# A hybrid attention / delta-rule layer on one core: streams woven in longer runs, two weight loads hoisted further, products of a constant at the start

## The chip, the cores and the metric

The kernel runs on one core of a Trainium2 chip. Its engines are TensorE (PE in the profile, with its weight loads as PEld), VectorE (DVE), ScalarE (ACT), GpSimd (POOL) and the engine whose queue issues most DMAs (SP). Each engine takes its instructions in the order in which the program lists them for that engine and waits where one needs a result of another. The metric is the device time of one execution in microseconds (us), lower is better.

## The reference

One layer over T = 1024 tokens of width D = 1024, all in float32. The input is normalised and multiplied by one wide matrix; its columns feed two mixers that run beside each other, and two gates merge them.

```python
h = rms_norm(x, pre_w)
proj = h @ w_in
# A: stick-breaking attention, 8 heads x 64, blocks of 128 queries
z = jnp.einsum('bhqd,bhkd->bhqk', qb, kb) * scale
log_keep = jnp.where(causal, -jax.nn.softplus(z), 0.0)
suffix = lax.cumsum(log_keep, axis=3, reverse=True) - log_keep
a = jnp.where(causal, jnp.exp(jax.nn.log_sigmoid(z) + suffix), 0.0)
o = jnp.einsum('bhqk,bhkd->bhqd', a, vb)
# B: conv(4) + SiLU on q, k, v, then a gated delta rule, 4 heads x 128, in chunks with a scan over them
merged = (jax.nn.sigmoid(merge_sb) * (o_sb @ w_branch_sb)
          + jax.nn.sigmoid(merge_gdn) * (o_g @ w_branch_gdn))
y = merged @ w_out
return x + rms_norm(y, post_w)
```

## The kernel before

**Dense tiles.** A product with a block of 128 columns of a weight matrix is made in two halves of 512 tokens. Weights and activations are split into a high and a low part, and of the four partial products three are made, over 8 blocks of the inner dimension: 24 matmuls of 512 columns for a half, into one of three PSUM tiles ("d"). `dense` (lines 204 to 214) is a generator that gives control back after every 3 matmuls and says that they cost 0.64. All other PSUM tiles, five of them, share one ring ("g"): the attention's scores z, transposes aT and results av are among them.

**Weights.** `load_w` (92 to 94) issues the DMA of a weight block (`raw`), ScalarE's copy that gives the high part (`whi`) and VectorE's subtraction that gives the low part (`wlo`). `tc.high_priority(offset=WPRI)` puts these three forward by 200 places of the program in the eyes of the framework's scheduler, which then fixes the order of each engine. Each of the three has two buffers.

**The stages by time.** 0 to 58 us: the rows of x are normalised, transposed on TensorE (xT, line 262), split into h_hi (ScalarE, 268) and h_lo (VectorE, 269), and the first two projections d_k (201) are made as the quarters of h become ready. 58 to 185 us: projections and preparation of the delta rule's first two heads (`g_mid(0)`); in its second half VectorE runs `lanes` (line 655 calls it), a chain of 62 dependent instructions (tmp, line 433, and a sum, line 435) whose size grows from one step to the next, and beside it TensorE makes dense tiles from `fill` (the merge gates, d_mg) and `g_gate` (d_gg). 185 to 245 us: the first scan, woven with two dense tiles. 245 to 368 us: `g_mid(1)`, the same for the other two heads, its lanes from about 306 to 356 us. 368 to 421 us: the second scan, woven with d_sk and d_sv. 421 to 489 us: more dense tiles and the branch product d_yb. 489 to 829 us: the attention, in four passes of two heads. 829 to 972 us: the branch product d_ya, the output product y (923), the last normalisation.

**The attention.** For every group of two query blocks `sb_z` (735 to 759) makes the scores in pieces of up to 512 columns (two matmuls each, 751 and 752); ScalarE makes two sigmoids of every piece (kp, bt; 754 and 755), VectorE runs a scan along kp (757) and GpSimd multiplies (758). `sb_av` (761 to 805), one group later, transposes blocks of bt (aT, line 774: four 128x128 transposes into one PSUM tile), has VectorE (779, 781) or ScalarE (783) copy them out, and multiplies pairs of blocks by the values (av, line 788), always one pair behind the transposes, except for a group's last pair. `weave` (233 to 243) joins this stream with the dense tiles of the next pass: at every step it runs the stream whose share of its stated cost is the smaller one, until that stream yields once.

Of the kernel before, what the change touches and what calls it, by code (L numbers as in the profile page):

```python
# [17 lines left out]
P = 128  # L18
# [2 lines left out]
CAP = 60.0  # L21
NSLOT = 23
AB = 4


@with_exitstack
def tile_stickbreak_gdn_hybrid(
# [15 lines left out]
    nc = tc.nc  # L43
# [3 lines left out]
    NP = 4  # L47
# [20 lines left out]
    def gps(name, shape=None):  # L68
        return psg.tile(shape or [P, 512], F32, tag="g", name=name)
# [20 lines left out]
        return hi, lo  # L90

    def load_w(src, nk, name):
        with tc.high_priority(offset=WPRI):
            return split_w(load_raw(src, nk, name), nk, name)

    WPRI = 200

    xs = []
    raw0 = []
# [52 lines left out]
    def rsqrt_act(dst, src, scale, bias, bias_f):  # L152
# [7 lines left out]
        nc.vector.tensor_mul(dst, dst, t)  # L160
        return sq

    epsb = const.tile([P, 1], F32, name="epsb")
    nc.vector.memset(epsb, EPS)
    prev_sq = [None]
# [58 lines left out]
    def chain(*gens):  # L224
        for g in gens:
            yield from g

    def drain(*gens):
        for g in gens:
            for _ in g:  # L230
                pass

    def weave(main, main_cost, side, side_cost):
        done = [0.0, 0.0]
        tot = [main_cost, side_cost]
        gens = [main, side]
        live = [True, True]
        while live[0] or live[1]:
            i = 0 if live[0] and (not live[1] or done[0] / tot[0] <= done[1] / tot[1]) else 1
            try:  # L240
                done[i] += next(gens[i])
            except StopIteration:
                live[i] = False

# [9 lines left out]
    for q in range(4):  # L254
        if q < 3:
            stats(q + 1)
        for k2 in range(NK // 2):
            ps = gps(f"xT_{q}_{k2}")
            for kk in range(2):
                for j in range(2):  # L260
                    k = k2 * 2 + kk
                    nc.tensor.transpose(ps[:, (kk * 2 + j) * P:(kk * 2 + j + 1) * P],
                                        xs[2 * q + j][:, k * P:(k + 1) * P], ident)
            qs = slice(q * QT, (q + 1) * QT)
            for kk in range(2):
                k = k2 * 2 + kk
                pk = ps[:, kk * QT:(kk + 1) * QT]
                ev = nc.scalar.mul(h_hi[:, k, qs], pk, prew[:, k:k + 1])
                nc.vector.scalar_tensor_tensor(h_lo[:, k, qs], pk, prew[:, k:k + 1], h_hi[:, k, qs].bitcast(F32),
                                               op0=ALU.mult, op1=ALU.subtract)  # L270
        if q < 2:
            hi = wp.tile([P, NK, P], F32R, tag="whi", name=f"whi_{first[q][1]}")
            lo = wp.tile([P, NK, P], F32R, tag="wlo", name=f"wlo_{first[q][1]}")
            nc.gpsimd.tensor_scalar(hi, raw0[q], 1.0, 1.0, op0=ALU.mult, op1=ALU.mult)
            nc.gpsimd.tensor_tensor(lo, raw0[q], hi.bitcast(F32), op=ALU.subtract)
            w0.append((hi, lo))
        todo = [(0, q)] if q < 2 else ([(1, 0), (1, 1), (0, 2), (1, 2)] if q == 2 else [(0, q), (1, q)])
        for i, qq in todo:
            ps = psd.tile([P, QT], F32, tag="d", name=f"d_{first[i][1]}_{qq}")
            dense_mm(ps, w0[i], NK, hk, qq * QT, (qq + 1) * QT)  # L280
            nc.scalar.copy(pre0[i][:, qq * QT:(qq + 1) * QT], ps)
# [140 lines left out]
    def lanes(b, lane_in):  # L422
        L = slot(f"L{b}", shape=[64, 32, 32])
        nc.sync.dma_start(L, lane_in.rearrange("h r c i j -> (h r c) i j"))
        nc.vector.tensor_scalar(L, L, -1.0, None, op0=ALU.mult)
        XL = slot(f"XL{b}", shape=[64, 32, 32])
        nc.gpsimd.memset(XL, 0.0)
        nc.gpsimd.affine_select(out=XL, in_=XL, pattern=[[1, 32], [-1, 32]], compare_op=ALU.not_equal, fill=1.0,
                                base=0, channel_multiplier=0)
        tmp = slot(f"tmp{b}")  # L430
        for i in range(1, 32):
            tv = tmp[:64, :i * i].rearrange("p (c j) -> p c j", j=i)
            nc.vector.tensor_tensor(tv, XL[:, 0:i, 0:i].rearrange("p j c -> p c j"),  # L433
                                    L[:, i:i + 1, 0:i].broadcast_to([64, i, i]), op=ALU.mult)
            nc.vector.tensor_reduce(XL[:, i, 0:i], tv, axis=AX.X, op=ALU.add)
        last = nc.vector.tensor_copy(L, XL.rearrange("p i j -> p j i"))
        lx = dram.tile([2, 4, NT, 32, 32], F32, name=f"lane_x{b}")
        lxt = dram.tile([2, 4, NT, 32, 32], F32, name=f"lane_xt{b}")
        nc.sync.dma_start(lx.rearrange("h r c i j -> (h r c) i j"), XL)
        nc.sync.dma_start(lxt.rearrange("h r c i j -> (h r c) i j"), L)  # L440
        lane_out[b] = lx, lxt
        return last
# [180 lines left out]
    def fill(n):  # L623
        for _ in range(n):
            if not gates:
                return
            m = gates.pop(0)
            wg = load_w(win[:, 4104 + m * P:4104 + (m + 1) * P], NK, f"mg{m}")
            gt = slot(f"mg_{m}")
            for half in range(2):  # L630
                hs = slice(half * HT, (half + 1) * HT)
                ps = yield from dense(wg, NK, hk, half, f"mg{m}")
                nc.scalar.activation(gt[:, hs], ps, AF.Sigmoid)  # L633
            nc.sync.dma_start(mg_d[m], gt)

    def g_mid(b, prev):
        h0, h1 = 2 * b, 2 * b + 1
        bs = slice(b * 16, b * 16 + 16)
        drain(g_q(h0))
        for h in (h0, h1):  # L640
            kn[h] = slot(f"kn_{h}", shape=[P, NT, P])
            sumsq(kT[h], ssk, h, f"k{h}", kn[h])
        li = g_m(b)
        drain(g_q(h1))
        for h in prev:
            g_o(h)
        sumsq(qT[h0], ssq, h0, f"q{h0}")
        g_i(h0)
        drain(g_v(h0))
        drain(g_v(h1))  # L650
        sumsq(qT[h1], ssq, h1, f"q{h1}")
        rsqrt(rqs[:, bs], ssq[:, bs], 1.0, 16)
        nc.vector.tensor_scalar(rqs[:, bs], rqs[:, bs], float(P) ** -0.5, None, op0=ALU.mult)
        g_i(h1)
        last = lanes(b, li)
        drain(fill(1))
        g_vt(h0)
        drain(fill(1))
        g_vt(h1)
        drain(fill(2), g_gate(h0), g_gate(h1))  # L660
        return chain(g_lev(h0, last), g_lev(h1, last), g_scan((h0, h1)))

    gates = gates[8:] + gates[:8]
# [175 lines left out]
    def until_none(g):  # L839
        for v in g:  # L840
            if v is None:
                return
            yield v

    for p in range(NP):
        side = chain(*[f(p + 1) for f in stages], fill(1)) if p + 1 < NP else fill(4)
        weave(until_none(att), 24.0, side, 52.0 if p + 1 < NP else 41.0)
    drain(fill(16), att)


# [120 lines left out]
```

## Time and profile before

| | |
|---|---|
| median of 3 runs | 977.01 us (977.01, 977.5, 972.46) |
| the profiled execution | 974.01 us |
| its span in the trace | 972.3 us |
| PE busy | 932.6 us, 96% of the span |
| VectorE, ScalarE, GpSimd busy | 628.3, 391.7, 192.6 us |
| attention, 489.3 to 829.4 us | 340.1 us, PE busy 333.2 us |

The span is what the trace covers; 1.7 us of the profiled execution lie around it. "Busy" leaves out waits. A row of the timeline gives the start of an instruction in us from the span's start and its length; a PE row's length includes the time in which it overlaps the next one, so the price of a matmul is read from start to start. In brackets stands how long the engine had been idle before it and what released it.

### The profile page before, as it was taken

To read this page: it belongs to the slowest core of one execution; us is meant where nothing else is said; L and a number is where in the kernel's file an instruction comes from. 1 tells how busy PE (TensorE), PEld (TensorE's weight loads), DVE (VectorE), ACT (ScalarE), POOL (GpSimd) and SP (SyncE) were. 2 spreads that over 40 slices of the span, in tenths; PEclk is the share of its full clock that TensorE was granted. 3 is DMA by queue.
4 is the path that set the end of the run, shared out by engine and by line. 5 is a ranking of instruction groups with operands and counts; after the bars stand their busy time and mean duration, and the time that the engine had idled before them with its cause. 6 is when DMAs were issued, how large, how long until landed. Compare 5 with 4: busy or idle time off the path is not lost.

```text
span 972.3 us, 13372 instructions
## 1 busy us (share of the span) xinstructions
PE 932.6 (96%) x5134; PEld 748.4 (77%) x5134; DVE 628.3 (65%) x1066; ACT 391.7 (40%) x861; POOL 192.6 (20%) x117
## 2 busy tenths in 40 slices
PE   4999999899999989999999999999999999999997
PEld 4968787688887767887887777777777777777886
DVE  6666899656899974656466635783774674563244
ACT  5665531235655212443254433552453443232221
POOL 4010210001103000000034312540632362341000
PEclk9999999999999989999999999999999999999999
DMA  8014222400242142004730111020011202671152
GB/s 262 7 41 118 77 65 86 110 23 23 66 109 66 66 112 40 12 23 155 246 109 22 44 44 43 22 66 23 22 43 44 77 33 65 246 269 70 46 196 106
DMA packets 88418, 80.12 MB, mean 82 GB/s; under 512 B 17097, under 2 KB 74530, under 8 KB 88354
## 3 DMA queue, kind: packets, MB, share of 16 engines
q1 hardware_dynamic: 86944, 79.20, 26.2%
q8 instruction: 40, 0.66, 0.3%
q10 hardware_dynamic: 1410, 0.07, 0.1%
q14 instruction: 24, 0.20, 0.1%
HBM read 60.88 MB, written 18.37 MB: 82 GB/s over the span
## 4 chain that ended last, share of the span: by engine, by line
PE 75%; DVE 15%; issue 4%; ACT 3%; POOL 2%; DMA 1%; SPq 0%; DVEq 0%; POOLq 0%; ACTq 0%
PE d_mg L211 12%; PE y L923 8%; PE d_sk L211 5%; PE d_sq L211 5%; PE d_sv L211 5%; PE d_yb L211 4%; PE d_q L211 4%; PE d_sgt L211 4%; PE av L788 4%; DVE tmp L433 3%; PE aT L774 3%; PE d_k L211 2%; PE d_gg L211 2%; PE d_k L201 2%; DVE kp L757 2%
## 5 line engine op out<-in xcount | busy, mean ns | idle before, releaser
L758 POOL TENSOR_TENSOR bt<-bt,kp 128x127 f32<-128x127 f32 (+3 forms) x64 | 123.1, 1941 | 381.0 <-DMA mb<-mg_d 164.9
L757 DVE TENSOR_TENSOR_SCAN kp<-kp,mscan 128x128 f32<-128x128 f32 (+3 forms) x64 | 105.5, 1673 | 30.2 <-ACT kp L754 29.9
L211 PE MATMUL d_mg<-h_hi,whi_mg 128*128 128x512 f32 x256 | 104.7, 409 | 0.2 <-ACT mg L633 0.2
L211 PE MATMUL d_mg<-h_hi,wlo_mg 128*128 128x512 f32 x256 | 100.8, 394 | 0.0
L211 PE MATMUL d_mg<-h_lo,whi_mg 128*128 128x512 f32 x256 | 100.1, 391 | 0.0
L754 ACT ACTIVATE kp<-z 128x384 f32<-128x384 f32 (+4 forms) x96 | 47.8, 499 | 71.6 <-PE z L752 67.3
L211 PEld LDWEIGHTS d_mg<-h_hi,whi_mg 128*128 128x128 f32 x256 | 48.2, 188 | 11.5 <-issue 3.4
L211 PEld LDWEIGHTS d_mg<-h_hi,wlo_mg 128*128 128x128 f32 x256 | 48.1, 188 | 10.5 <-issue 0.2
L211 PEld LDWEIGHTS d_mg<-h_lo,whi_mg 128*128 128x128 f32 x256 | 48.2, 188 | 7.6
L923 PE MATMUL y<-wohi,m_hi 128*128 128x512 f32 (+1 forms) x136 | 52.0, 383 | 1.2 <-ACT m_hi L879 1.2
L755 ACT ACTIVATE bt<-z 128x384 f32<-128x384 f32 (+4 forms) x96 | 47.7, 498 | 11.7 <-DMA mB_d<-mb 5.4
L923 PE MATMUL y<-wohi,m_lo 128*128 128x512 f32 (+1 forms) x136 | 52.0, 382 | 0.4 <-DVE m_lo L880 0.4
L923 PE MATMUL y<-wolo,m_hi 128*128 128x512 f32 (+1 forms) x136 | 51.8, 381 | 0.0
L433 DVE TENSOR_TENSOR tmp<-XL,L 64x1 f32<-64x1 f32 (+30 forms) x62 | 47.7, 769 | 1.6
L788 PE MATMUL av<-aT,svn 128*64 128x256 f32 (+1 forms) x320 | 39.6, 370 | 6.7 <-DVE aT L779 3.6
L774 PEld LDWEIGHTS aT<-ident,bt 128*128 128x128 f32 x288 | 35.6, 140 | 10.4 <-issue 0.8
L774 PE MATMUL aT<-ident,bt 128*128 128x128 f32 x288 | 43.5, 273 | 0.2 <-ACT bt L755 0.2
L356 POOL TENSOR_TENSOR acc_k<-acc_k,pre_k 128x1024 f32<-128x1024 f32 x4 | 9.6, 2390 | 157.9 <-ACT pre_k L355 136.9
L788 PEld LDWEIGHTS av<-aT,svn 128*64 128x64 f32 x320 | 19.8, 136 | 25.6 <-issue 15.5
L927 ACT ACTIVATE yj<-y 128x512 f32<-128x512 f32 (+1 forms) x17 | 9.7, 573 | 66.9 <-PE y L923 64.4
L211 PE MATMUL d_gg<-h_hi,wlo_gg 128*128 128x512 f32 x64 | 26.5, 414 | 9.4 <-DVE wlo_gg L89 9.4
L895 POOL TENSOR_TENSOR sA<-sA,mBl 128x512 f32<-128x512 f32 x16 | 24.7, 1557 | 47.8 <-DVE sA L894 45.7
(377 smaller groups left out, 2468.6 us busy)
## 6 DMA issues: line engine op xcount, KB each, us to landing
raw_mg<-in_w_in_dram SPq DMA_DIRECT2D x16, 512.0 KB, 4.0
mg_d<-mg SPq DMA_DIRECT2D x16, 512.0 KB, 3.0
x<-in_x_dram SPq DMA_DIRECT2D x8, 512.0 KB, 6.4
mb<-mg_d SPq DMA_DIRECT2D x8, 512.0 KB, 6.8
mB_d<-mb SPq DMA_DIRECT2D x8, 512.0 KB, 4.2
sA<-mg_d SPq DMA_DIRECT2D x8, 512.0 KB, 7.2
mBl<-mB_d SPq DMA_DIRECT2D x8, 512.0 KB, 6.1
rawo<-in_w_out_dram SPq DMA_DIRECT2D x8, 512.0 KB, 4.6
```

Of the source, the lines that this page charges most:

```text
L201: nc.tensor.matmul(ps, lhsT=a[:, k], rhs=b[:, c0:c1], start=(k == 0 and i == 0), stop=(k == nk - 1 and i == 2))
L211: nc.tensor.matmul(ps, lhsT=a[:, k], rhs=b[:, hs], start=(k == 0 and i == 0), stop=(k == nk - 1 and i == 2))
L433: nc.vector.tensor_tensor(tv, XL[:, 0:i, 0:i].rearrange("p j c -> p c j"), L[:, i:i + 1, 0:i].broadcast_to([64, i, i]), op=ALU.mult)
L754: nc.scalar.activation(kp[:, os_], ps[:, :pc], AF.Sigmoid, scale=-0.125)
L755: nc.scalar.activation(bt[:, os_], ps[:, :pc], AF.Sigmoid, scale=0.125)
L757: nc.vector.tensor_tensor_scan(kp[:, :n], kp[:, :n], mscan[:, :n], 1.0, op0=ALU.mult, op1=ALU.max)
L758: nc.gpsimd.tensor_tensor(bt[:, 1:n], bt[:, 1:n], kp[:, 0:n - 1], op=ALU.mult)
L774: nc.tensor.transpose(ps[:, (a * 2 + j) * P:(a * 2 + j + 1) * P], at[p, a, qb][:, off:off + P], ident)
L788: nc.tensor.matmul(av[a * 64:(a + 1) * 64, j0 * P:2 * P], lhsT=vn[:, c, a * 64:(a + 1) * 64], rhs=aT[:, a * 2 + j0:a * 2 + 2], start=(c == ...
L895: nc.gpsimd.tensor_tensor(ga[:, hs], ga[:, hs], mb[:, hs], op=ALU.add)
L923: nc.tensor.matmul(ps, lhsT=a[:, k, ts_], rhs=b[:, c0:c1], start=(k == 0 and i == 0), stop=(k == NK - 1 and i == 2))
L927: nc.scalar.activation(junk.rearrange("p a b -> p (a b)")[:, :c1 - c0], ps, AF.Square, accum_out=ss)
```

## The change

It has three parts. First, `weave` takes two numbers, and lets a stream go on until it has done that much more of its stated cost: 1.9 for both streams in the two scans; in the attention 1.9 for the attention's own stream and 5.0 for the dense one, which is a whole half of a dense tile (8 x 0.64 = 5.12). Second, `load_w` reads its offset from `ahead`; in `g_mid` it is 600 instead of 200 between the call of `lanes` and the end of the dense tiles beside it. Third, `keep_awake` multiplies a 128x128 matrix of ones by itself into a PSUM tile that nothing reads: 18 times at the beginning, and 6 times each behind two of the first quarter's four groups of transposes.

```diff
+RUN = 1.9
+HALF = 5.0
...
     def load_w(src, nk, name):
-        with tc.high_priority(offset=WPRI):
+        with tc.high_priority(offset=ahead[0]):
             return split_w(load_raw(src, nk, name), nk, name)
 
-    WPRI = 200
+    ahead = [200]
...
+    def keep_awake(n, after=None):
+        with ExitStack() as held:
+            if after is not None:
+                held.enter_context(tc.issue_after(after.ins))
+            ps = gps("awake")
+            for i in range(n):
+                nc.tensor.matmul(ps[:, :P], lhsT=ones, rhs=ones, start=True, stop=True)
+
+    keep_awake(18)
...
-    def weave(main, main_cost, side, side_cost):
+    def weave(main, main_cost, side, side_cost, runs=(RUN, RUN)):
...
             try:
-                done[i] += next(gens[i])
+                upto = done[i] + runs[i]
+                while done[i] < upto:
+                    done[i] += next(gens[i])
             except StopIteration:
                 live[i] = False
...
                     k = k2 * 2 + kk
-                    nc.tensor.transpose(ps[:, (kk * 2 + j) * P:(kk * 2 + j + 1) * P],
+                    xt_ = nc.tensor.transpose(ps[:, (kk * 2 + j) * P:(kk * 2 + j + 1) * P],
                                         xs[2 * q + j][:, k * P:(k + 1) * P], ident)
+            if q == 0 and k2 % 2:
+                keep_awake(6, xt_)
...
         last = lanes(b, li)
+        ahead[0] = 600
         drain(fill(1))
...
         drain(fill(2), g_gate(h0), g_gate(h1))
+        ahead[0] = 200
...
-        weave(until_none(att), 24.0, side, 52.0 if p + 1 < NP else 41.0)
+        weave(until_none(att), 24.0, side, 52.0 if p + 1 < NP else 41.0, (RUN, HALF))
```

The lines of the attention lie 17 further down in the changed kernel (774 is 791, 788 is 805, 751 is 768), those of `dense` 11 (211 is 222).

On TensorE, in a pass of the attention beside the dense tile d_mg, the order before has a product of three between the transposes of one block (aT_2_4) and the products av of the pair before:

```order
L774 MATMUL aT_2_4_5779<-ident,bt_0_4_5443 128x128
L774 MATMUL aT_2_4_5779<-ident,bt_0_5_5479 128x128
L774 MATMUL aT_2_4_5779<-ident,bt_1_4_5502 128x128
L774 MATMUL aT_2_4_5779<-ident,bt_1_5_5522 128x128
L211 MATMUL d_mg_1_5752<-h_hi,whi_mg_5683 128x512
L211 MATMUL d_mg_1_5752<-h_lo,whi_mg_5683 128x512
L211 MATMUL d_mg_1_5752<-h_hi,wlo_mg_5684 128x512
L788 MATMUL av_2_5740<-aT,svn_4866 64x256 x4
```

Here is the same place on TensorE in the changed kernel, from the last matmul of a dense half on:

```order
L222 MATMUL d_mg_1_5799<-h_hi,wlo_mg_5731 128x512
L791 MATMUL aT_2_4_5824<-ident,bt_0_4_5479 128x128
L791 MATMUL aT_2_4_5824<-ident,bt_0_5_5493 128x128
L791 MATMUL aT_2_4_5824<-ident,bt_1_4_5507 128x128
L791 MATMUL aT_2_4_5824<-ident,bt_1_5_5521 128x128
L805 MATMUL av_2_5776<-aT,svn_4913 64x256 x4
L791 MATMUL aT_2_3_5835<-ident,bt_0_4_5479 128x128
L791 MATMUL aT_2_3_5835<-ident,bt_0_5_5493 128x128
```

All 24 matmuls of the half now stand ahead of aT_2_4, and none between it and av. Over the attention, TensorE's list before has 396 unbroken stretches of one kind (dense, scores, transposes, av), of which 38 are av blocks; after, 159, of which 32 are av blocks. Of the 40 pairs of av, 11 had less than 1.4 us of TensorE work between their own last transposes and them before and the others 2.5 to 6 us; after, 14 have less than 2.3 us and the other 26 have 5.9 us or more (counted in the two orders, with the start-to-start times of the trace). Runs of scores reach 7 pieces, four times.

On VectorE, near the end of the second lanes (tmp and the sum XL, of growing size), the order before puts the low part of the fourth head's gate weights behind the last sum:

```order
L433 TENSOR_TENSOR tmp_2925<-XL_2920,L_2917 64x900
L435 TENSOR_REDUCE XL_2920<-tmp_2925 64x30
L433 TENSOR_TENSOR tmp_2925<-XL_2920,L_2917 64x961
L435 TENSOR_REDUCE XL_2920<-tmp_2925 64x31
L89 TENSOR_TENSOR wlo_gg_3324<-raw_gg_3321,whi_gg_3323 128x1024
L436 COPY L_2917<-XL_2920 64x1024
```

The changed kernel has VectorE make it two instructions earlier:

```order
L448 TENSOR_TENSOR tmp_2958<-XL_2953,L_2950 64x900
L450 TENSOR_REDUCE XL_2953<-tmp_2958 64x30
L91 TENSOR_TENSOR wlo_gg_3357<-raw_gg_3354,whi_gg_3356 128x1024
L448 TENSOR_TENSOR tmp_2958<-XL_2953,L_2950 64x961
L450 TENSOR_REDUCE XL_2953<-tmp_2958 64x31
L451 COPY L_2950<-XL_2953 64x1024
```

The third head's wlo_gg moves in the same way, from behind the sum of size 26 to between tmp of size 625 and the sum of size 25. In the first lanes the two keep their places.

On TensorE at the start, the order before goes from the last transposes of the first quarter (x_85 and x_87 are its two tiles) to three products of d_k, and then on to the second quarter's first transpose (x_91):

```order
L262 MATMUL xT_3_227<-ident,x_85 128x128
L262 MATMUL xT_3_227<-ident,x_87 128x128
L201 MATMUL d_k_0_240<-h_hi,whi_k_236 128x256
L201 MATMUL d_k_0_240<-h_lo,whi_k_236 128x256
L201 MATMUL d_k_0_240<-h_hi,wlo_k_237 128x256
L262 MATMUL xT_0_292<-ident,x_91 128x128
```

The changed kernel has six products of ones there, and then d_k without a transpose between its products:

```order
L275 MATMUL xT_3_253<-ident,x_85 128x128
L275 MATMUL xT_3_253<-ident,x_87 128x128
L171 MATMUL awake<-ones 128x128 x6
L212 MATMUL d_k_0_273<-h_hi,whi_k_269 128x256
L212 MATMUL d_k_0_273<-h_lo,whi_k_269 128x256
L212 MATMUL d_k_0_273<-h_hi,wlo_k_270 128x256
```

All 24 products of d_k's first quarter now precede the second quarter's 16 transposes, which before lay among them. Six more products of ones stand between the first quarter's second and third group of transposes, 18 ahead of everything. In the two scans TensorE's order is the same in both kernels; GpSimd's order is the same throughout.

## Rows read from the trace of the kernel before

**Rows 1.** The page's head and its first part: busy time, share of the span and number of instructions of each engine.

```profile
span 972.3 us, 13372 instructions
PE 932.6 (96%) x5134; PEld 748.4 (77%) x5134; DVE 628.3 (65%) x1066; ACT 391.7 (40%) x861; POOL 192.6 (20%) x117
```

**Rows 2.** The table of stretches: start and end, length, then busy us and number of instructions of PE, PEld, DVE, ACT and POOL, the clock that TensorE was granted (1.00 is the upper of its two levels), the DMA engines' share and GB/s. A stretch behind the second lanes, and the attention.

```profile
353.70:360.60 6.90, 5.44 (x13) 4.28 (x14) 5.31 (x7) 0.00 (x0) 0.00 (x0) 0.51 0.67 159
489.30:829.40 340.10, 333.23 (x1776) 258.86 (x1774) 206.17 (x203) 148.82 (x294) 119.71 (x59) 1.00 0.16 48
```

**Rows 3.** The table of waits of the whole span: who waited for whom, us in total, times, the longest.

```profile
PE d_gg L211 <- DVE wlo_gg L89: 9.4, 4, 3.8
...
PE av L788 <- DVE aT L779: 3.6, 3, 1.4
...
PE av L788 <- DVE aT L781: 3.1, 2, 1.8
...
PEld av L788 <- issue: 15.5, 26, 2.2
```

**Rows 4.** The timeline of PE alone, at one av block that stands between dense matmuls, and at the attention's very end, where av and transposes follow each other.

```profile
516.62 0.39 PE L211 MATMUL d_sv<-h_lo,whi_sv 128*128 128x512 f32 x1
516.85 0.39 PE L211 MATMUL d_sv<-h_hi,wlo_sv 128*128 128x512 f32 x1
517.16 1.08 PE L788 MATMUL av<-aT,svn 128*64 128x256 f32 x8
518.18 0.50 PE L211 MATMUL d_sv<-h_hi,whi_sv 128*128 128x512 f32 x1
518.52 0.40 PE L211 MATMUL d_sv<-h_lo,whi_sv 128*128 128x512 f32 x1
...
823.88 1.08 PE L788 MATMUL av<-aT,svn 128*64 128x256 f32 x8
824.89 1.09 PE L774 MATMUL aT<-ident,bt 128*128 128x128 f32 x8
...
827.74 1.74 PE L788 MATMUL av<-aT,svn 128*64 128x256 f32 x16
829.40 0.50 PE L211 MATMUL d_ya<-oshi,whi_wbs 128*128 128x512 f32 x1
```

**Rows 5.** The timeline of all engines around one wait of av in the third pass: the low part of a weight and a scan on VectorE, the transposes, the copy, and av.

```profile
597.13 1.66 DVE L89 TENSOR_TENSOR wlo_sq<-raw_sq,whi_sq 128x1024 fp32r<-128x1024 f32 x1 [0.51 <-ACT whi_sq L88]
...
598.71 2.03 DVE L757 TENSOR_TENSOR_SCAN kp<-kp,mscan 128x512 f32<-128x512 f32 x1
...
599.02 0.38 PE L774 MATMUL aT<-ident,bt 128*128 128x128 f32 x2
...
600.66 0.99 DVE L779 TENSOR_TENSOR aT<-aT,mdiag 128x512 f32<-128x512 f32 x2
...
601.47 0.76 PE L788 MATMUL av<-aT,svn 128*64 128x256 f32 x6 [1.36 <-DVE aT L779]
```

**Rows 6.** The attention's groups of the same line and shape, 489.3 to 829.4 us: count, busy us, mean ns of one, idle before. The scores' two sigmoids of 384 columns; then, of line 757, all scans with the shortest, median and longest in ns.

```profile
L754 ACT ACTIVATE kp<-z 128x384 f32<-128x384 f32 x23 | 11.5, 502 | 15.0 <-PE z L752 14.9
L755 ACT ACTIVATE bt<-z 128x384 f32<-128x384 f32 x23 | 11.5, 499 | 0.0
...
L757 DVE TENSOR_TENSOR_SCAN kp<-kp,mscan x59: 418/1731/4411, 494.0 to 800.1; 128x512 f32<-128x512 f32 x8, 128x640 f32<-128x640 f32 x8, 128x768 f32<-128x768 f32 x8, 128x896 f32<-128x896 f32 x8
```

**Rows 7.** The timeline of VectorE and of PE in the second lanes.

```profile
334.53 1.31 DVE L433 TENSOR_TENSOR tmp<-XL,L 64x625 f32<-64x625 f32 x1
...
338.94 1.21 DVE L89 TENSOR_TENSOR wlo_gg<-raw_gg,whi_gg 128x1024 fp32r<-128x1024 f32 x1
...
340.20 0.50 PE L211 MATMUL d_gg<-h_hi,wlo_gg 128*128 128x512 f32 x1 [1.30 <-DVE wlo_gg L89]
...
349.85 1.08 DVE L435 TENSOR_REDUCE XL<-tmp 64x30 f32<-64x900 f32 x1
...
353.89 1.21 DVE L89 TENSOR_TENSOR wlo_gg<-raw_gg,whi_gg 128x1024 fp32r<-128x1024 f32 x1
...
355.16 0.79 PE L211 MATMUL d_gg<-h_hi,wlo_gg 128*128 128x512 f32 x1 [3.78 <-DVE wlo_gg L89]
355.75 0.63 PE L211 MATMUL d_gg<-h_hi,whi_gg 128*128 128x512 f32 x1
...
360.44 0.46 PE L211 MATMUL d_gg<-h_hi,wlo_gg 128*128 128x512 f32 x1
360.75 0.40 PE L211 MATMUL d_gg<-h_hi,whi_gg 128*128 128x512 f32 x1
```

**Rows 8.** The timeline of the start: the row of x that the first transposes wait for, those transposes, d_k's wait and the last transposes of the second quarter. The last two rows are of the first scan: a product of two 128x128 float32 matrices, which the trace shows as two records, and the instruction behind it.

```profile
9.48 2.94 DVE L179 TENSOR_SCALAR x<-x,rx 128x1024 f32<-128x1024 f32 x1
...
12.48 2.82 PE L262 MATMUL xT<-ident,x 128*128 128x128 f32 x12 [3.44 <-DVE x L179]
...
17.91 0.38 PE L201 MATMUL d_k<-h_lo,whi_k 128*128 128x256 f32 x1 [1.73 <-DVE h_lo L269]
...
21.28 0.93 PE L262 MATMUL xT<-ident,x 128*128 128x128 f32 x7
...
205.64 0.38 PE L554 MATMUL Sn<-vs,kn 128*128 128x128 f32 x2
205.85 0.39 PE L549 MATMUL vnew<-vb,Xt 128*128 128x128 f32 x2
```

## The prediction

> **What bounds the kernel now.** I read the busy table first. TensorE works 932.6 of 972.3 us, and no other engine comes near [rows 1]: so a microsecond counts only where TensorE waits, or where it is slower than it could be. The table of waits shows where it waits [rows 3]: 9.4 us in four waits for the low part of a gate weight (d_gg), 6.7 us in five waits of av for VectorE's copies of the transposes (3.6 and 3.1). The last row there is of the weight loads: before 26 of av's 320, the loader stood still for 15.5 us with nothing to wait for. The table of stretches adds the clock [rows 2]: it is at the upper level in the attention, and 0.51 in the 6.9 us behind the second lanes. Of the attention's 340.1 us TensorE is busy 333.2; the rest is nearly all av's five waits.
>
> **The attention: fewer switches.** A step in a dense run is 0.23 us (516.62 to 516.85) [rows 4]. The block of eight av between 516.85 and 518.52 takes 1.67 us with two dense steps in it, so 1.67 - 2 x 0.23 = 1.21 us. What the eight need by themselves comes from the attention's end: eight take 1.01 us (823.88 to 824.89), sixteen, of which four are half as wide, 1.66 us (827.74 to 829.40), so six full ones more take 0.65 us, 0.108 each, and eight 0.87. Coming from dense work and going back to it thus costs 1.21 - 0.87 = 0.34 us. The order has 38 av blocks before and 32 after: 6 x 0.34 = **2.0 us less**. The many fewer switches between dense work and scores or transposes I count at nothing: I found no such loss at them in the rows. The ends of this term are 2.0 and, by the row of the loader (15.5 us in 26 blocks, 0.6 each), 3.6 us.
>
> [...]
>
> **The attention: av's old waits.** One of the five [rows 5]: the transposes are done at 599.4, but VectorE has a weight's low part (1.66 us) and a scan (2.03 us) in hand, begins the copy at 600.66, and av starts at 601.47, 1.36 us late. There was little between the transposes and av. Now a whole dense half of 24 x 0.23 = 5.5 us stands ahead of 26 of the 40 pairs of av. The same queue (1.66 + 2.03 us) and the copy (0.99 us) make 4.7 us, less than that. So these waits go: **6.7 us less**; bounds 0 and 6.7.
>
> **The attention: what is late next.** Three things. (1) 14 pairs keep less than 2.3 us of cover, three more than before had less than 1.4; each with one scan ahead of its copy (median 1.73 us [rows 6]) could wait up to about 1 us. (2) Runs of scores are longer. A piece of 384 columns needs two sigmoids of 0.50 us on ScalarE [rows 6], where TensorE makes it in some 0.35 us (two matmuls, three quarters of a dense step each). With five PSUM tiles in the ring, one of them held by av, a piece can start when the fourth before it has been read: the sixth waits until 0.35 + 2 x 1.0 = 2.35 us instead of 1.75, the seventh until 3.35 instead of 2.70, together 1.25 us. Four such runs cost 5 us, and 2.6 if the two sigmoids overlap a little (0.8 us a piece). (3) GpSimd and VectorE get their work in bursts, but the results are wanted only one group later. I take **3 us more**, near the lower price of the runs, and keep 0 and 8 (5 of the runs, 3 of the short covers) as ends. The attention together: -2.0 - 6.7 + 3 = -5.7 us, and from -10 to +6 between the ends.
>
> **The second lanes.** For the third head, VectorE begins wlo_gg at 338.94 and TensorE starts at 340.20, 1.30 us late, so it was there at 338.90. Now wlo_gg follows tmp of size 625, which ends at 335.84 [rows 7]; it is ready at 337.1: this wait goes, 1.3 us. For the fourth head, wlo_gg now follows the sum that ends at 350.93, not the one at 353.9, and is ready at 352.15. TensorE came to it at 355.16 - 3.78 = 351.38, and with the 1.3 us won, at 350.08; it waits 2.1 us instead of 3.8. It starts at 352.2 in place of 355.16: **2.9 us less**, both waits together. VectorE's chain itself ends at the same time as before, since it only takes the two subtractions earlier; what depends on its end (the loads of the lanes' result) is not later. Queued behind the two subtractions are the chain's next steps, 1.2 us later each, and nothing else waits for those. Then the clock: from 355.75 to 360.44 a step takes 0.43 us and from 360.75 on 0.23, in the stretch with clock 0.51 [rows 2, 7]. That is 13 steps at 0.2 us, 2.6 us. Whether a wait of 2.1 us brings the same drop no row shows: I take half, **1.3 us less**, with ends 0 and 2.6. The term is -4.2; its ends are -5.5, and 0 if the scan behind it, which needs the lanes' result, waits for what was won. The two waits in the first lanes (the rest of the 9.4 us) stay, since the order there is unchanged.
>
> **Hoisting on the queues.** The higher offset issues a handful of loads on SP's queue one place earlier. SP's queue has nothing there that TensorE waits for [rows 3], so I count nothing; bounds of -0.5 and +0.5.
>
> **The start.** The 18 first products stand ahead of work that waits for x: TensorE's first long row begins at 12.48, after 3.44 us idle behind VectorE's 2.94 us row [rows 8]. A product of two float32 matrices of 128x128 takes 0.21 us (205.64 to 205.85), and twice that at the lower level: 18 are 3.8 to 7.6 us, and fit into the idle time. The other 12 products lie on the path: 2.5 us, or 5.0 at the lower level. Against that stand the 1.73 us for which d_k waited for h_lo at 17.91, which the products now partly fill, so 0.8 to 3.3 us more. If TensorE were at its upper level already at 12.48, the first quarter's 14 remaining transposes would take 0.13 us each as in the row at 21.28 (0.93 for 7) instead of 0.23 (2.82 for 12), 1.4 us less: the lower end is -0.6. The second quarter's transposes now come behind all of d_k's first quarter, and with them ScalarE's and VectorE's split of that quarter; TensorE has d_k's other tile for the first quarter to do meanwhile (24 products), so I count nothing for it, with +1 as its end. I take **1.5 us more**, with ends -0.6 and +4.3.
>
> **The sum**, against the profiled execution (974.0 us, 972.3 in the span): -5.7 - 4.2 + 1.5 = -8.4, so 965.6 us. That execution is 3.0 us below the median of the runs shown, and the four times average 975.2; the like of that average is **967 us**.
>
> **Rivals.** (a) *The gain stays away.* The attention's waits only change their place: av's copies come late for the 14 short covers and the scores wait for PSUM, in all as much as the 6.7 us before. Then -2.0 + 3 (runs) + 0, lanes -2.9 without the clock, start +2.5: +0.6, about 976. For it speaks that VectorE is 61% busy in the attention (206.2 of 340.1 us [rows 2]), against it that 26 pairs get a cover longer than the queue seen at a wait. (b) *Slower: VectorE's bursts.* With scores in runs, two or three scans stand together in VectorE's queue, in front of the copies for av. The longest scan took 4.41 us [rows 6]; two such and a low part of 1.66 us are 10.5 us, 5 us more than the dense half covers. It decides from about 5.5 us of queue on. Once in each pass would be 4 x 5 = 20 us: -8.4 - 3 + 20 = +8.6, about 984. Against it speaks that the longest is two and a half times the median. [...] (d) *The products at the start don't do what they are named for:* they leave the clock as it was and cost their whole 4.3 us; 970 with the rest as forecast.
>
> **How the numbers follow.** A measurement of this kernel can tell about 0.5%, 4.9 us, from no change: faster is below 972.1, slower above 981.9. Forecast 0.50, (a) 0.26, (b) 0.11, (c) 0.05, (d) 0.08. The forecast's own range is 961 to 972, from the lanes' and the attention's middle ends. (c) and (d) are also faster, if little: with a quarter of (d) and a tenth of the forecast going to "same", faster has 0.45 + 0.05 + 0.06 = 0.56; same 0.05 + 0.02 + 0.24 of (a) = 0.31; slower (b) and the rest of (a), 0.13. The range is 958 to 979: the good ends of attention and lanes below, (a) with a bad start above; (b) lies outside.
>
> **What would show it.** In the changed profile: av's waits for aT gone or below 2 us in the table of waits (else (a)); no wait of av above 3 us (else (b)); the third head's wait for wlo_gg gone and the fourth's near 2.1 us, and whether the clock behind it stays up; scores waiting for ScalarE, 3 us in all; d_k's first product behind the last products of ones at about 16 to 18 us, and h ready 1 to 2 us later. The forecast is wrong if the attention takes more than 337 us, or if the start loses more than 4 us.

## The result and the profile after

The changed kernel takes 980.12 us (median of 8 runs, 978.11 to 982.7), against 975.31 us for the kernel before in the same comparison (8 runs): the ratio is 1.0058 with a 95% interval of [1.0042, 1.0074]. It is slower by 0.6%, where I had forecast 967 us and a range up to 979. The profiled execution took 980.29 us.

The page's head and first part of the changed kernel answer to [rows 1]:

```profile
span 978.6 us, 13475 instructions
...
PE 942.0 (96%) x5194; PEld 763.8 (78%) x5194; DVE 626.1 (64%) x1066; ACT 386.7 (40%) x861; POOL 192.6 (20%) x117
```

The span is 6.3 us longer; TensorE is busy 9.4 us more. Of these, 7.8 us lie before the logits, where the change gives TensorE 60 more records, the 30 products of ones, and 2.5 us in the attention, where the number of records is the same. A matmul at the lower clock is longer, and so counts as more busy time: a step of d_mg takes 0.23 us at 312.36 us, where the clock is 1.00, and 0.43 at 317.43, where it is 0.50. The busy share hides such a loss. The table of waits of the changed kernel's TensorE answers to [rows 3]:

```profile
PE av L805 <- DVE aT L796: 6.9, 5, 2.5
PE d_gg L222 <- DVE wlo_gg L91: 4.2, 2, 2.6
...
PE d_mg L222 <- ACT mg L648: 3.9, 1, 3.9
PE t_q L379 <- ACT jk L381: 2.2, 1, 2.2
PE av L805 <- DVE aT L798: 2.0, 3, 0.9
...
PE aT L791 <- ACT bt L772: 1.1, 2, 0.7
```

The waits for wlo_gg fell from 9.4 to 4.2 us, but a wait of d_mg for ScalarE is new (3.9), one of t_q grew from 0.8 to 2.2, and av waits 8.9 us for its copies, not 6.7. Where the time went by stages comes from the times at which TensorE reaches the same points in both traces: 0.8 us later when it begins the logits (46 us), 3.3 us later at the end of the first lanes, 1.2 us at the end of the second (so these gave 2.1 back), 1.1 us at the attention's start, 7.2 us at its end, and 6.3 us at the last product. Nearly all of it arises in the attention. (Behind it the changed kernel's trace makes up 0.9 us: the trace of the kernel before stands at 0.50 for 3.4 us from 882.8 us on and loses 1.7 us by it, and this one does not fall there.) The table of stretches shows it, with the attention first, then four short ones and the one that stood at 0.51 in [rows 2]:

```profile
490.20:836.60 346.40, 335.77 (x1776) 266.55 (x1774) 201.65 (x203) 143.99 (x294) 120.71 (x59) 0.99 0.16 48
651.00:657.00 6.00, 4.58 (x27) 4.26 (x28) 4.75 (x9) 2.09 (x9) 1.59 (x3) 0.72 0.40 110
741.00:750.00 9.00, 7.29 (x34) 6.31 (x35) 6.28 (x10) 2.60 (x9) 2.33 (x4) 0.62 0.23 62
174.00:180.00 6.00, 3.92 (x11) 3.17 (x12) 5.97 (x7) 0.40 (x1) 0.00 (x0) 0.72 0.46 138
315.00:323.00 8.00, 6.16 (x16) 4.87 (x17) 7.55 (x21) 2.75 (x4) 0.00 (x0) 0.57 0.44 132
353.70:360.60 6.90, 6.90 (x33) 5.69 (x32) 6.80 (x6) 1.80 (x3) 0.00 (x0) 1.00 0.18 45
```

The attention takes 346.4 us, 6.3 more than before. Two stretches in it stand partly at 0.50, the lower of the two levels in these traces, at the end of the second pass (653.5 to 656.9 us) and of the third (742.2 to 749.0); they lose 6.0 x 0.28 + 9.0 x 0.38 = 5.1 us. Behind the second lanes the clock is now at 1.00, but it fell to 0.50 at 315.6 us instead, in the new wait of d_mg. The fall in the stretch at 174 us comes at 175.6 us, in the first lanes' wait of 2.58 us for wlo_gg, which the kernel before has too (2.60 us), without a fall. The timeline of TensorE, VectorE and GpSimd at the end of the third pass shows what precedes such a fall:

```profile
735.14 0.66 PE L791 MATMUL aT<-ident,bt 128*128 128x128 f32 x4 [0.70 <-ACT bt L772]
736.28 1.08 PE L805 MATMUL av<-aT,svn 128*64 128x256 f32 x8 [0.48 <-DVE aT L798]
737.30 0.87 PE L791 MATMUL aT<-ident,bt 128*128 128x128 f32 x6
739.09 1.08 PE L805 MATMUL av<-aT,svn 128*64 128x256 f32 x8 [0.92 <-DVE aT L798]
742.72 1.55 PE L805 MATMUL av<-aT,svn 128*64 128x256 f32 x8 [2.54 <-DVE aT L796]
...
736.16 2.29 DVE L774 TENSOR_TENSOR_SCAN kp<-kp,mscan 128x1024 f32<-128x1024 f32 x1
738.38 0.66 DVE L798 COPY aT<-aT 128x512 f32<-128x512 f32 x1
738.96 3.10 DVE L91 TENSOR_TENSOR wlo_mg<-raw_mg,whi_mg 128x1024 fp32r<-128x1024 f32 x1
741.98 1.01 DVE L796 TENSOR_TENSOR aT<-aT,mdiag 128x512 f32<-128x512 f32 x2
...
738.62 2.35 POOL L775 TENSOR_TENSOR bt<-bt,kp 128x1023 f32<-128x1023 f32 x1 [5.19 <-ACT aT L800]
```

No dense product stands between these rows. The stream's last transposes are done at about 738.2; VectorE copies the first of them, then makes the low part of a weight that only the next pass needs, and only then the last two copies. That low part takes 3.10 us, and GpSimd's product runs beside it for 2.0 us; the 40 low parts of this size that have no work of GpSimd beside them in this trace take 1.20 to 1.23 us each. TensorE stands idle for 4.6 us in four pieces, and the eight av behind the last take 1.55 us; the same eight at the end of the second pass (652.42 us), where the clock fell only behind them, at 653.5, take 0.87. There, at 652 us, the same wait stands behind the low part wlo_sv.

The kernel before, at the end of its third pass:

```profile
732.99 1.52 PE L788 MATMUL av<-aT,svn 128*64 128x256 f32 x12
735.00 0.40 PE L211 MATMUL d_mg<-h_lo,whi_mg 128*128 128x512 f32 x1
735.32 0.44 PE L788 MATMUL av<-aT,svn 128*64 128x128 f32 x4
...
732.88 0.69 DVE L779 TENSOR_TENSOR aT<-aT,mdiag 128x512 f32<-128x512 f32 x1 [1.44 <-PE aT L774]
733.48 1.22 DVE L89 TENSOR_TENSOR wlo_mg<-raw_mg,whi_mg 128x1024 fp32r<-128x1024 f32 x1
734.62 0.42 DVE L779 TENSOR_TENSOR aT<-aT,mdiag 128x256 f32<-128x256 f32 x1
...
731.02 2.41 POOL L758 TENSOR_TENSOR bt<-bt,kp 128x1023 f32<-128x1023 f32 x1 [2.70 <-DVE kp L757]
```

The low part stands among the last copies here too. But it takes 1.22 us, with GpSimd's product over at 733.43, and two matmuls of scores and two dense ones stand on TensorE between the last av and those ahead of it, so TensorE does not wait.

### The profile page after: what moved, and what is told of

Its sections match the earlier page's. It is cut to its first block, busy times and chain, and to the rows that moved or that the text cites. A ratio compares the mean times of both kernels' runs of the same rounds, so it can differ in the third digit from the quotient of the medians.

```text
span 978.6 us, 13475 instructions
## 1 busy us (share of the span) xinstructions
PE 942.0 (96%) x5194; PEld 763.8 (78%) x5194; DVE 626.1 (64%) x1066; ACT 386.7 (40%) x861; POOL 192.6 (20%) x117
## 4 chain that ended last, share of the span: by engine, by line
PE 78%; DVE 12%; issue 4%; ACT 3%; POOL 2%; DMA 0%; DVEq 0%; POOLq 0%; ACTq 0%
PE d_mg L222 11%; PE y L940 8%; PE d_sk L222 5%; PE d_sv L222 5%; PE d_v L222 4%; PE d_sq L222 4%; PE d_q L222 4%; PE d_yb L222 4%; PE d_sgt L222 3%; PE d_gg L222 3%; PE av L805 3%; PE aT L791 3%; PE d_k L222 2%; PE d_k L212 2%; DVE tmp L448 2%
## 5 line engine op out<-in xcount | busy, mean ns | idle before, releaser
L771 ACT ACTIVATE kp<-z 128x384 f32<-128x384 f32 (+4 forms) x96 | 50.0, 521 | 77.3 <-PE z L769 72.4
L772 ACT ACTIVATE bt<-z 128x384 f32<-128x384 f32 (+4 forms) x96 | 50.8, 529 | 8.6 <-DMA mB_d<-mb 5.6
L791 PE MATMUL aT<-ident,bt 128*128 128x128 f32 x288 | 40.8, 287 | 1.5 <-ACT bt L772 1.1
L91 DVE TENSOR_TENSOR wlo_mg<-raw_mg,whi_mg 128x1024 fp32r<-128x1024 f32 x16 | 23.5, 1467 | 16.0 <-ACT whi_mg L90 16.0
```

Of the source, the lines that this page charges most:

```text
L91: nc.vector.tensor_sub(lo[:, :nk], raw[:, :nk], hi[:, :nk].bitcast(F32))
L771: nc.scalar.activation(kp[:, os_], ps[:, :pc], AF.Sigmoid, scale=-0.125)
L772: nc.scalar.activation(bt[:, os_], ps[:, :pc], AF.Sigmoid, scale=0.125)
L791: nc.tensor.transpose(ps[:, (a * 2 + j) * P:(a * 2 + j + 1) * P], at[p, a, qb][:, off:off + P], ident)
```

## The experiments

Theory A was that the whole loss lies at these two ends of passes: the long halves had used up the dense work that covered them before, the low part of the next weight stands in VectorE's queue ahead of the last copies, and the clock falls behind the wait. Theory B was that the start and the hoisted loads cost it. Each ratio below is to the kernel before on the same chip.

**The attention woven step by step again (u_att).** In the changed kernel:

```diff
-        weave(until_none(att), 24.0, side, ..., (RUN, HALF))
+        weave(until_none(att), 24.0, side, ..., (0.01, 0.01))
```

> The changed kernel with the attention woven step by step as before; the hoisted loads and the products of ones stay. Theory A (the loss of 5 us comes from the long dense halves: they leave the end of the second and third pass without dense work, av waits there behind a low part on VectorE, and the clock drops behind the wait): about 974 us, attention back to 340 us, no stretch at the lower clock in it. Theory B (the loss is spread over the start and the hoisted loads, and the halves are harmless): 979 to 980.

Measured: 974.38 us, ratio to before 0.9987 [0.9970, 1.0005]. The attention takes 340.3 us again. As theory A had it: the loss comes with the longer runs in the attention; the other two parts together neither gain nor lose enough to be told. The edit undoes both numbers there, 1.9 for the attention's own stream and 5.0 for the dense one, so which of the two it is isn't shown.

**Without the hoist (u_hoist), and without the products of ones (u_awake).** Two runs:

```diff
-        ahead[0] = 600
+        ahead[0] = 200
```

> The changed kernel with the offset of 200 everywhere. By the times at which TensorE reaches the same points in the two traces, the hoist costs 2.5 us in the first lanes and gives 2.1 in the second. Theory A: within 1 us of the changed kernel, 979 to 981. Theory B (the hoisted loads are a good part of the loss): 976 or less. My prediction had the hoist at 4.2 us of gain; by that it would be 984.

```diff
-    keep_awake(18)
...
-            if q == 0 and k2 % 2:
-                keep_awake(6, xt_)
```

> The changed kernel without any product of ones. Theory A: 0.8 us less than the changed kernel (the delay of TensorE at 40 us in the traces), about 979.3. Rival: they raise the clock and so help: 981 or more. My prediction had them at 1.5 us of cost: 978.6.

Measured: 982.18 us without the hoist, 1.0066 [1.0042, 1.0090]; 979.94 us without the products, 1.0048 [1.0032, 1.0064]. Neither can be told from the changed kernel's 1.0058 [1.0042, 1.0074]: these parts don't make the loss, and the products of ones do nothing that shows. In both traces TensorE stands idle about as long at the ends of the second and the third pass as in the changed kernel's: 3.1 us of the six from 648 us on, where that has 3.1, and 3.8 us (u_hoist) and 3.6 (u_awake) of the nine from 738 on, where it has 3.5. Both show the clock at the lower level at both ends, for 3.4 or 6.8 us each; of the runs that follow, which move or fill that wait or weave step by step, none shows a fall in the attention: its rows of 3 us all read 1.00.

**The low parts behind the last copies (low_behind).** The last copy for av of a pass's third group is remembered, and every later low part is ordered behind it. Over the attention seven low parts change their place on VectorE; at each of the two ends two now stand behind the copies, of which one had been among them. TensorE's order stays but for one instruction's place.

```diff
+    mask = [None]
...
+        with ExitStack() as held:
+            if mask[0] is not None:
+                held.enter_context(tc.issue_after(mask[0].ins))
-        nc.vector.tensor_sub(lo[:, :nk], raw[:, :nk], hi[:, :nk].bitcast(F32))
+            nc.vector.tensor_sub(lo[:, :nk], raw[:, :nk], hi[:, :nk].bitcast(F32))
...
-                nc.vector.tensor_tensor(dst, src, mdiag[:, :, 0:2 - j0], op=ALU.mult)
+                mk = nc.vector.tensor_tensor(dst, src, mdiag[:, :, 0:2 - j0], op=ALU.mult)
+                if c == cl and g == 2:
+                    mask[0] = mk
```

> The changed kernel with one edit: the low part of the next pass's weights, which VectorE made between the copies for av at the end of a pass, is ordered behind the last of those copies. TensorE's order and the long halves stay. Theory A, with the clock drop as a result of the wait: the two waits of av of 2.5 us and the two drops behind them (5 us together) go, about 970. The wait alone, with a clock that drops anyway: 975. Theory B, or the halves costing by themselves: 979 to 980.

Measured: 968.2 us, 0.9929 [0.9901, 0.9957], the changed kernel turned from a loss into a gain of 0.7%. The timeline of the same place, and the attention's stretch:

```profile
733.84 0.88 PE L796 MATMUL aT<-ident,bt 128*128 128x128 f32 x6
735.64 1.74 PE L812 MATMUL av<-aT,svn 128*64 128x256 f32 x16 [0.92 <-DVE aT L805]
...
734.91 0.67 DVE L805 COPY aT<-aT 128x512 f32<-128x512 f32 x1
735.50 1.01 DVE L801 TENSOR_TENSOR aT<-aT,mdiag 128x512 f32<-128x512 f32 x2
736.42 3.33 DVE L94 TENSOR_TENSOR wlo_mg<-raw_mg,whi_mg 128x1024 fp32r<-128x1024 f32 x2
...
492.10:827.60 335.50, 330.90 (x1777) 262.68 (x1775) 199.44 (x203) 143.86 (x294) 120.61 (x59) 1.00 0.17 49
```

The copies now precede the low parts, the 2.54 us wait before the last av is gone, and the clock reads 1.00 in the attention, which takes 335.5 us: 10.9 less than in the changed kernel and 4.8 less than before. TensorE is busy 4.9 us less in it than in the changed kernel's attention (330.90 and 335.77) for the same work, near the 5.1 us that the two stretches at the lower clock lost.

**The wait filled (fill_wait).** The same place in the changed kernel, with the wait left as it is, but 12 products of ones for TensorE in it, before the last pair of av:

```diff
+        tail = [None]
...
-                nc.tensor.matmul(av[a * 64:(a + 1) * 64, j0 * P:2 * P], lhsT=vn[:, c, a * 64:(a + 1) * 64],
+                tail[0] = nc.tensor.matmul(av[a * 64:(a + 1) * 64, j0 * P:2 * P], lhsT=vn[:, c, a * 64:(a + 1) * 64],
...
+        if g == 2 and p in (1, 2):
+            keep_awake(12, tail[0])
         for e in q:
             mm(*e)
```

> The changed kernel with 12 products of ones more at two places: on TensorE between the av blocks where it stood idle for 2.5 us at the end of the second and the third pass. The wait itself stays; 12 x 0.21 = 2.5 us of work that nobody reads fill it. Theory A (the clock falls because TensorE stands idle there): the two stretches at the lower clock (1.7 and 3.4 us lost) stay away and nothing else changes, about 975 us. Rival (the clock falls for another reason, and the products only lengthen the path): 980 to 982.

Measured: 975.73 us, 1.0010 [0.9993, 1.0026], 4.4 us below the changed kernel. The attention's stretch and TensorE at 650 us (a product of ones is two records):

```profile
490.60:832.90 342.30, 336.75 (x1824) 267.98 (x1822) 200.84 (x203) 143.67 (x294) 122.50 (x59) 1.00 0.16 49
...
650.15 2.94 PE L171 MATMUL awake<-ones 128*128 128x128 f32 x24
653.02 0.87 PE L807 MATMUL av<-aT,svn 128*64 128x256 f32 x8
```

The products fill 2.9 us where TensorE stood idle, and the clock reads 1.00 in the attention, which takes 4.1 us less than in the changed kernel, with the copies as late as there. So of the 10.9 us between the changed kernel and low_behind, 4 to 5 are the clock and the other 6 to 7 mostly the waits themselves. At these two places the clock fell with TensorE idle, and read 1.00 with the products there (640 to 660 and 736 to 752 us).

**Are the halves worth anything (step_low)?** The kernel low_behind, with the attention woven step by step by the edit of u_att:

> The kernel low_behind with the attention woven step by step, as before the change; so the low part is ordered behind the last copies, but there are no whole halves. Theory A (the halves themselves remove the five old waits of av and some switches, worth 5 us; only the pass ends spoiled it): about 973, near u_att. Rival (the place of the low part is the whole gain, the halves do nothing): 968.

Measured: 972.71 us, 0.9976 [0.9961, 0.9991]. The attention takes 339.1 us and av still waits 6.4 us for its copies, so the place of the low parts is not the gain (against u_att it can't be told from nothing); it lets the halves' gain stand.

**The halves alone (halves_low).** low_behind with the two edits of u_hoist and u_awake added:

> The kernel low_behind without the hoist (offset 200 everywhere) and without the products of ones: of the change only the longer runs are left, with the low part behind the last copies. By the runs u_hoist and u_awake the two other parts are worth about 1 to 2 us and nothing: 969 to 970. If the hoist were worth the 4.2 us of my prediction: 972.

Measured: 968.23 us, 0.9939 [0.9916, 0.9962]: the same as low_behind.

**Low parts behind the copies of every group (low_all).** In low_behind:

```diff
-                if c == cl and g == 2:
+                if c == cl:
```

> The kernel low_behind with the low parts ordered behind the last copy for av of every group, not only of the third. 3.5 us of waits of av for copies are left in low_behind, by its trace. If low parts cause them, 966. Rival: these waits come from scans, and low parts that come later make dense work wait: 968 or more.

Measured: 977.65 us, 1.0035 [1.0021, 1.0050]: worse than low_behind by about 9 us, more than the rival said. TensorE's waits in it:

```profile
PE d_ya L227 <- DVE sA L918: 2.8, 2, 1.9
...
PE d_ya L227 <- DVE wlo_wbs L94: 1.5, 1, 1.5
PE d_sgt L227 <- DVE wlo_sgt L94: 1.4, 2, 0.7
...
PE d_sq L227 <- DVE wlo_sq L94: 1.1, 2, 0.6
```

Dense work now waits for its low parts, and av's waits have shrunk by 0.8 us only. These waits make 4.0 us. By place, 5.3 us of the 9 lie in the attention, which takes 340.8 us; which part of the rest is TensorE's order, which also changed, is not shown.

**The hoist alone (hoist_only).** The kernel before, with the change's second part (`ahead`, and 600 between `lanes` and the last `drain` of `g_mid`) and no other:

```diff
+        ahead[0] = 600
...
+        ahead[0] = 200
```

> The kernel before with the hoist alone: offset 600 behind the lanes, nothing else. My prediction counted 4.2 us of gain (two waits shorter by 2.9 us together, half of a clock drop), so about 970. By u_hoist and halves_low it is worth between nothing and 2 us, so 972 to 974; in the trace the waits for wlo_gg are 4.2 instead of 9.4 us, a wait of d_mg for ScalarE of 3.9 us is new, and a stretch at the lower clock stands behind that one instead of behind the second lanes.

Measured: 973.56 us, 0.9986 [0.9970, 1.0002], against 974.87 for the kernel before: 1.4 us less by the ratio, not told from nothing, and not the 4.2 of the prediction. Its waits for wlo_gg are 4.2 us, that of d_mg for ScalarE 4.1 and that of t_q 2.2, as in the changed kernel.

**The waits in the lanes filled (lanes_fill).** halves_low with products of ones where TensorE waits for wlo_gg; the waits stay:

```diff
+WAITS = {'gg0': 7, 'gg1': 11, 'gg2': 5, 'gg3': 16}
...
-                nc.tensor.matmul(ps, lhsT=a[:, k], rhs=b[:, hs], start=(k == 0 and i == 0),
+                mm_ = nc.tensor.matmul(ps, lhsT=a[:, k], rhs=b[:, hs], start=(k == 0 and i == 0),
...
+                if k == 0 and half == 0 and i == 1 and name in WAITS:
+                    keep_awake(WAITS[name], mm_)
```

> The kernel halves_low with products of ones in the four waits of TensorE for wlo_gg (7, 11, 5 and 16 of them at 0.21 us, about as long as the waits of 1.7, 2.6, 1.3 and 3.8 us); the waits stay. If the clock falls because TensorE stands idle there, the two stretches at the lower clock in the lanes (1.7 and 3.4 us lost in halves_low) go: 963 to 964. If the clock falls anyway, or the delay is made up for behind the lanes: 968.

Measured: 966.34 us, 0.9906 [0.9883, 0.9928], against 968.23 for halves_low: 1.9 us by the medians, less than the 4 to 5 expected, though the profiled executions differ by 5.1. The span and mean granted clock of its trace:

```profile
core 0: 964.6 us, clock 0.999
```

The table of stretches shows no fall before the last product: every row reads 1.00. (The page's row of the clock in tenths can't tell: in the kernel before it reads 9 in the slice of the fall at 882.8 us too.)

The profiled execution of halves_low is the slowest of its six (971.38 us, the others 967.3 to 970.6), with a stretch at the lower clock at the start, from the row at 15 us on, that loses 3.4 us, and a mean clock of 0.989, the others 0.992 to 0.994; that is why I trust the medians for the size. This is the fastest version by its median, though its interval overlaps those of halves_low and low_behind; it leaves out the hoist and the products at the start, and has products of ones where a wait is known.

## Why the prediction was wrong

**What bounds the kernel** was right: in these runs the time moved with TensorE's waits, its clock and its switches. But I counted a fall of the clock in one place alone, the lanes.

**Fewer switches** (2.0 us forecast): about the right size. In low_behind av, the transposes and the scores wait 4.5 us where before it was 6.9, which is 2.4 of the 4.8 us that the attention gained; the other 2.4 us are what is left over for the switches. TensorE's busy time agrees, 330.9 us against 333.2, both at a clock of 1.00 and for the same matmuls. That it is av's six blocks, as the term had it, and not the many other switches that went, is not shown. That switches cost nothing, which is (c) among the forecast's chances with its 0.05, no run shows; what the runs showed in its place are these 2.3 us.

**av's old waits** (6.7 us): right in mechanism. Where a half stands ahead of av, three waits of 0.6 us are left in the trace of low_behind in place of the five, so 4.9 of the 6.7 us went. In step_low they are still there (6.4 us).

**What is late next** (3 us): here the step failed, its point (1). I saw that 14 pairs of av keep less than 2.3 us of cover, and priced them with "one scan ahead" at "up to about 1 us" each. At two of them VectorE had a scan, a copy and a low part of 3.10 us (1.66 in [rows 5]) ahead of the last copies, so TensorE stood for 3.3 us at the first and 4.6 us at the second end; and behind it the clock fell, a term that I had for the lanes and left out here. In place of 3 us of waits the attention has 10.6 (6.9 before), and 5.1 us of clock on top: -2.4 for the switches, +3.7 and +5.1 make the 6.4 us that it lost. With the low parts moved, the attention gained 4.8 us against the forecast's 5.7. The longer runs of scores (2), for which I had most of the 3 us, showed no wait worth a row.

Rival (a), whose waits only change their place to the short covers, had the place right; at 976 it priced them at the old 6.7 us, where 8.9 us of av's waits came, and had no clock in it. Rival (b), slower through VectorE's bursts, came as near in time (984 against 980.1), but its place was wrong: it set the point of decision at a queue longer than a dense half covers, and the loss arose where no half was left. What I missed can be read in the changed order: VectorE's list there has the low part between the copies, as before, and TensorE's no longer has a dense row beside them. I had counted covers on TensorE's list, and not looked at what stands on VectorE's list within the short ones. That the low part would take 1.9 us longer there, beside GpSimd's product, no list shows; how much of the loss that alone is, no run tells.

**The lanes** (4.2 us): the two waits of the second lanes went, also the 2.1 us that I had left for the fourth head (none of the 4.2 us left for wlo_gg is there). But the step "I count nothing" for the hoist's effect on the queues failed. The higher offset moves d_mg's loads forward too: ScalarE now has a high part whi_mg, for which it waits 4.63 us, in front of the work on D (L400) and the copy of pre_v that VectorE needs, where before it stood behind D. VectorE then waits 1.63 us for that copy, and the first step of the lanes' chain comes 5.9 us later than before, of which the stage's own late start explains about 3. TensorE meets a new wait of 3.9 us for ScalarE instead:

```profile
292.43 1.05 ACT L90 CAST whi_mg<-raw_mg 128x1024 fp32r<-128x1024 f32 x1 [4.63 <-PE d_v L222]
...
298.80 3.34 DVE L366 TENSOR_SCALAR acc_v<-pre_v,par 128x1024 f32<-128x1024 f32 x1 [1.63 <-ACT pre_v L364]
...
311.59 1.28 ACT L400 ACT_TABLE_LOAD   x1 [3.41 <-DVE D1.0_3_2927 L399]
312.89 1.06 ACT L400 ACTIVATE D1.0_3_2927<-D1.0_3_2927 128x1024 f32<-128x1024 f32 x1
313.85 1.03 ACT L90 CAST whi_mg<-raw_mg 128x1024 fp32r<-128x1024 f32 x1
...
316.19 1.57 ACT L648 ACTIVATE mg<-d_mg 128x512 f32<-128x512 f32 x3
...
316.84 0.79 PE L222 MATMUL d_mg<-h_hi,whi_mg 128*128 128x512 f32 x1 [3.86 <-ACT mg L648]
317.43 0.63 PE L222 MATMUL d_mg<-h_lo,whi_mg 128*128 128x512 f32 x1
317.86 0.63 PE L222 MATMUL d_mg<-h_hi,wlo_mg 128*128 128x512 f32 x1
```

ScalarE waits for VectorE's D until 311.59; the copy of d_mg out of PSUM (L648) stands behind that, and TensorE behind the copy. A step of d_mg then takes 0.43 us: the clock fell here, to 0.50 from 315.6 to 322.4 us, and not behind the second lanes, so that half of a clock drop was no gain either. The first lanes, which I had said stay, also became 2.5 us longer. In all, by hoist_only, 1.4 us [-0.2, 2.9] of 4.2.

**The start** (1.5 us more): within its ends, but too much. TensorE's rows at the start of the changed kernel:

```profile
12.31 1.54 PE L275 MATMUL xT<-ident,x 128*128 128x128 f32 x6 [3.96 <-DVE x L190]
13.65 2.23 PE L171 MATMUL awake<-ones 128*128 128x128 f32 x12
15.72 1.04 PE L275 MATMUL xT<-ident,x 128*128 128x128 f32 x8
16.59 1.50 PE L171 MATMUL awake<-ones 128*128 128x128 f32 x12
17.85 0.37 PE L212 MATMUL d_k<-h_hi,whi_k 128*128 128x256 f32 x1
```

The products take 3.3 us, but d_k's wait for h_lo at 17.91 in [rows 8] is taken up by them, and the eight transposes at 15.72 take 0.11 us from one to the next, where those at 12.31 need 0.22. As at the term's lower end, the one pays for the other: u_awake shows no difference. The 18 products at the beginning do not keep the clock up in this trace: TensorE then stands idle for 3.96 us for x, the table of stretches has the clock at 0.50 from 12 to 15 us, and the transposes at 12.31 are as slow as those at 12.48 in [rows 8].

## What to carry to other kernels

Where work is woven to cover a wait, look for the places where the covering stream has ended: here the longer pieces removed 4.9 us of waits in the middle, and 7.9 us of idle time came at two ends, where the other engine's list had a low part of 3.10 us between a result and its reader. These waits of TensorE cost more than their length, as the clock fell with them: 5.1 us of clock came on top of the 7.9. Moving a few instructions that nothing needed yet turned a loss of 0.6% into a gain of 0.7%, and filling a wait that stayed with products that nobody reads won back 4.4 us.

## What the runs showed of the hardware that I had not expected

TensorE's clock fell behind or in an idle time of 2.54 us with two or three shorter ones (0.21 to 0.92 us) in the seven us before it, at both pass ends in the changed kernel's trace; u_hoist and u_awake, idle about as long there, show a fall at both ends too. Single waits of 0.8 to 1.8 us in the attention of the kernel before were not followed by a fall: its clock reads 1.00. How long an idle time must be the runs do not show. The kernel before itself has a fall at 882.8 us, behind waits of 1.18 and 0.40 us, and the wait of 2.6 us for wlo_gg at the end of the first lanes has one in the changed kernel (at 175.6 us) and none in the kernel before, u_att and hoist_only, whose rows there read 1.00. With products of ones in the waits (fill_wait, lanes_fill) it did not fall there, and in lanes_fill nowhere before the last product: the rows read 1.00.

At the start, the seven traces of kernels with the products of ones at the beginning all show a fall between 10 and 19 us, and of the five without them only halves_low does. But the table's clock is not to be relied on there: in the kernel before it reads 1.00 from the first row on, while its transposes take 0.23 us each at 12.48 and 0.13 at 21.28 [rows 8].
